# Splitting two mixer outputs during the attention, and another order of rows in the output projection

## The chip, the cores and the metric

The kernel runs on one core of a Trainium2 chip. The metric is the device time of one execution in microseconds (us). TensorE is PE in the views (its weight loads PEld), VectorE DVE, ScalarE ACT, GpSimd POOL, and SyncE, which issues most loads, SP.

## What is computed

A transformer of two layers over 512 tokens of width 1024, in float32. In each layer an input projection feeds three mixers: a sparse attention (512 columns), a gated delta net (256) and a convolution branch called conformer (256). Their outputs are joined and projected, and a mixture of 32 experts follows.

```
y_nsa  = _nsa(q, k_cmp, ..., gates, ...)
y_gdn  = _gated_deltanet(gdn_qkv, gdn_z, gdn_b, gdn_a, ...)
y_conf = _conformer_conv(conf_in, ...)
mix = jnp.concatenate([y_nsa, y_gdn, y_conf], axis=-1) @ w_out[l]
x = _layer_norm(DEEPNORM_ALPHA * x + mix, ln1_w[l], ln1_b[l])
moe = _hier_moe(x, ...)
x = _layer_norm(DEEPNORM_ALPHA * x + moe, ln2_w[l], ln2_b[l])
```

## The kernel before

Each layer has three stages. In the **mixer stage** the string `ORDER` gives the order in which the steps are written down: `k`, `c`, `q` are input projections, `w` to `z` prepare the queries of the four token tiles, `0` to `3` are their attention, `f` and `t` the conformer, and each `G` is one piece of the delta net, whose last pieces stand at the end. The **output projection** follows (L1104 to L1159), then routing and the **expert stage**, whose weights (6 MB for an expert) SP loads into rings of buffers. The experts are taken in an order that routing finds: the load of a routed expert needs its id, which SP reads from the tile `r_id` (L1247). Two experts are fixed and are loaded before.

Dependencies, semaphores and the order on each engine are not written by hand. A planner goes through the program and, by a model of the times, gives each engine its queue: of what is ready it takes what stands first in the program. On the chip each queue runs in that order. Tiles of one tag share a number of buffers, and a tile takes one when the planner comes to its first write and one is free. A pool that is opened where another one was closed waits for the old tiles that its own lie over.

The mixer outputs are four tiles of 128 x 1024: `mxA[0]` and `mxA[1]` (attention; token tiles 0 and 1, and 2 and 3), `mxC` (conformer, made in step `t`) and `mxG` (delta net). Products here are made of float32r halves: a value is split into a `hi` part by a cast on ACT and a `lo` part, the difference, by a subtraction on DVE (or POOL), and `mm3` (L354) makes three matmuls, hi x hi (L355), hi x lo (L356) and lo x hi (L357).

Before the projection a loop (L1105 to L1110) splits all four outputs. Its `hi` tiles (`mh`) lie in the pool `out`, and so do the six buffers for the split weights (`wo_hi`, `wo_lo`, tag `whl`); this pool takes over the space of the delta net's pool `g`, which is full of its 10 wide tiles (tag `g4`), the last of them `g_o`. The `lo` tiles (`ml`) take over buffers of the tags `cf` and `mxA`.

The projection then runs for two pairs of token tiles. Each goes through the 1024 rows of `w_out` in four quarters of 256 rows (`kq`), each a load of 1 MB on SP into a ring of three buffers, and each quarter in two parts of 128 rows, `k` = 2 `kq` and 2 `kq` + 1. A part is split (cast on ACT, L1132; subtraction on POOL for `k` in 1, 4, 7, else on DVE, L1133), and 12 matmuls follow: 2 token tiles x 2 halves of the columns x 3. Rows 0 to 511 (`k` 0 to 3) belong to the attention, `k` 4 and 5 to the delta net, 6 and 7 to the conformer. The quarters come in this order:

```
kq = (2, 3, 0, 1)[i]
```

so the delta net's rows are first. The sums lie in the banks of `opA` and `opB`; those of `opA` are the ones in which the delta net had `g_mix`, the transposes (L716) from which `mxG` is evacuated. After each pair come the residual with `xr`, a norm and the routing's logits.

The wide tiles of tag `x4` share six buffers: `cvt` (conformer), `kva0` and `kva1` (keys and values, read to the end of the attention), `kk` (compression), `q0` and `q1`, later the four `xr` (the residual, loaded on ACT's queue at L1115) and the two `xg` (gathered tokens, filled with zeros on POOL at L1198).

Of the kernel before, what the change touches and what calls it, by code (L numbers as in the profile page):

```python
# [21 lines left out]
D = 1024  # L22
NT = 4
P = 128
# [88 lines left out]
def hybrid_kernel(ctx, tc, x_in, w_in, w_out, cmp_pe, cmp_w1, cmp_w2, conv_w, a_log, dt_bias, norm_w,  # L113
# [191 lines left out]
    for l in range(layers):  # L305
# [492 lines left out]
        cvt = x4("cvt")  # L798
        for step in ORDER:
# [11 lines left out]
            elif step == 'k':  # L811

                kva = [x4(f"kva{i}") for i in range(2)]
# [34 lines left out]
            elif step == 'm':  # L848
# [7 lines left out]
                for kind in range(2):  # L856
# [3 lines left out]
                    if kind == 0:  # L860
                        kk = x4("kk")
# [33 lines left out]
            elif step == 'q':  # L895

                qq = [x4(f"q{i}") for i in range(2)]
# [18 lines left out]
            elif step == 't':  # L916
                mxC = conformer_tail(ca)
            elif step == 'r':
# [184 lines left out]

        mh, ml = [], []  # L1104
        for src, tag in ((mxC, "cf"), (mxA[0], "cf"), (mxA[1], "mxA"), (mxG, "mxA")):  # L1105
            hi, lo = tp("out", "mh", 4, dt=F32R), tp("mix", tag, 2, "ml", F32R)
            A.copy(hi, src)
            V.tensor_tensor(lo, src, hi.bitcast(F32), op=ALU.subtract)
            mh.append(hi)
            ml.append(lo)  # L1110
        mh, ml = [[m[i] for i in (3, 0, 1, 2)] for m in (mh, ml)]
        for pr in range(2):
# [4 lines left out]
            def lt(m, k, t):  # L1117
                if k < 4:
                    return m[2 + t // 2][:, (t % 2) * 512 + k * P:(t % 2) * 512 + (k + 1) * P]
                return m[(k - 4) // 2][:, (k % 2) * 512 + t * P:(k % 2) * 512 + (t + 1) * P]  # L1120

            ap = [bank2("opA"), bank2("opB")]
            for i in range(4):
                kq = (2, 3, 0, 1)[i]
                w = wring("w_out")
                nc.sync.dma_start(w.rearrange("p (k c) -> p k c", k=2),
                                  w_out[l, kq * 256:(kq + 1) * 256, :].rearrange("(k p) c -> p k c", p=P))
                for kk in range(2):
                    k = 2 * kq + kk
                    src = w[:, kk * 1024:(kk + 1) * 1024]  # L1130
                    hi, lo = tp("out", "whl", WL, "wo_hi", F32R), tp("out", "whl", WL, "wo_lo", F32R)
                    A.copy(hi[:, :1024], src)  # L1132
                    (G if k in (1, 4, 7) else V).tensor_tensor(lo[:, :1024], src, hi[:, :1024].bitcast(F32), op=ALU.subtract)  # L1133
                    for t in (2 * pr, 2 * pr + 1):
                        for n in range(2):
                            mm3(ap[t % 2][:, n, :], lt(mh, k, t), lt(ml, k, t), hi[:, n * 512:(n + 1) * 512],
                                lo[:, n * 512:(n + 1) * 512], i == 0 and kk == 0, i == 3 and kk == 1)
# [504 lines left out]
```

## Time and profile before

| | |
|---|---|
| three runs | 1964.27, 1965.96 (median), 1978.44 us |
| the profiled execution | 1966.44 us, its span 1964.7 us |
| busy share of the span | PE 89%, DVE 51%, ACT 29%, POOL 20% |
| mean TensorE clock granted | 0.923 of full speed |
| HBM read | 476 MB, 247 GB/s over the span |

The span goes from the first to the last instruction of the profiled execution; all times in the rows count from its start. Layer 0 has its output projection from 371 to 425 us, layer 1 from 1345 to 1400. In a timeline a row gives start, duration, engine, line, operation, the tiles written and read, and in brackets how long the engine had been idle and what ended that. PEclk is the granted clock of TensorE: 1.00 is 2.4 GHz, 0.50 is 1.2 GHz. Matmuls are pipelined: a row's 0.39 us is longer than the pitch at which rows follow each other.

### The profile page before, as it was taken

The numbers are of one execution on the slowest core, as the hardware profiler recorded it, in microseconds if no ns is written. First come the engines' busy times: TensorE is split into PE (matmuls) and PEld (weight loads), VectorE is DVE, ScalarE is ACT, GpSimd is POOL, SyncE is SP. The second block draws the span as 40 slices with busy tenths as digits, with TensorE's granted clock in tenths as the row PEclk, the third lists the DMA queues.
The fourth block names the chain that finished last, engine by engine and source line by source line (L and its number), as shares of the span: only waits on it lengthen the run. The fifth ranks groups of instructions, "written<-read, shape, count | busy, mean of one in ns | idle before, by whom it ended". The sixth has DMA issues, their size and how long they took to land. (4 is left out here: it accounts for less than half of the span.)

```text
span 1964.7 us, 31355 instructions
## 1 busy us (share of the span) xinstructions
PE 1743.3 (89%) x11812; PEld 1021.7 (52%) x11812; DVE 1009.4 (51%) x2258; ACT 573.8 (29%) x1250; POOL 387.3 (20%) x354
## 2 busy tenths in 40 slices
PE   8899699887988899999789987998799898999996
PEld 6776576672443434333377765666634434343333
DVE  2756867463533524343637659664644324244335
ACT  3332565432110112121233336553222101121122
POOL 2224641312200000000222356213131000000001
PEclk9997689988999899999999976998889998999998
DMA  5222000747999989999632210017489999799994
GB/s 179 87 86 76 12 12 12 264 152 284 408 402 405 403 323 383 409 374 409 249 110 82 90 64 2 12 43 267 138 320 409 402 403 405 305 399 408 362 409 181
DMA packets 147339, 478.41 MB, mean 244 GB/s; under 512 B 23032, under 2 KB 25584, under 8 KB 147184
## 3 DMA queue, kind: packets, MB, share of 16 engines
q1 hardware_dynamic: 138304, 456.74, 61.0%
q10 hardware_dynamic: 4144, 10.70, 1.5%
q0 software_dynamic: 4736, 8.92, 1.3%
q8 instruction: 95, 1.56, 0.3%
q14 instruction: 60, 0.49, 0.1%
HBM read 476.04 MB, written 8.39 MB: 247 GB/s over the span
## 5 line engine op out<-in xcount | busy, mean ns | idle before, releaser
L1282 PE MATMUL f_gu<-w_gu,m_xe 128*32 128x256 f32 (+1 forms) x3456 | 398.6, 454 | 19.9 <-DMA w_gu<-in_moe_w_up 17.8
L1282 PEld LDWEIGHTS f_gu<-w_gu,m_xe 128*32 128x32 f32 (+1 forms) x3456 | 134.9, 118 | 270.6 <-issue 222.5
L1314 PE MATMUL f_y<-w_d,f_hTs 128*32 128x256 f32 (+2 forms) x1824 | 258.1, 480 | 9.9 <-ACT f_hTs L1299 2.9
L1324 DVE TENSOR_TENSOR m_yl<-f_y,m_yh 32x256 fp32r<-32x256 f32 (+2 forms) x222 | 115.3, 520 | 263.8 <-ACT m_yh L1322 256.1
L1322 ACT CAST m_yh<-f_y 32x256 fp32r<-32x256 f32 (+2 forms) x222 | 98.4, 443 | 304.0 <-PE f_y L1314 301.7
L1374 POOL DMA_INDIRECT xg<-x1D,m_idx x34 | 35.9, 1056 | 744.3 <-PE f_hT L1297 331.2
L1314 PEld LDWEIGHTS f_y<-w_d,f_hTs 128*32 128x32 f32 (+2 forms) x1824 | 83.5, 126 | 162.0 <-issue 130.8
L1435 DVE TENSOR_TENSOR xr<-xr,m_sc 128x1024 f32<-128x1024 f32 x128 | 152.8, 1218 | 25.5 <-PE m_sc L1434 24.6
L1289 DVE SCALAR_TENSOR_TENSOR f_h<-f_h,m_wsl,f_gu 128x128 f32<-128x128 f32 (+1 forms) x76 | 33.0, 434 | 227.1 <-ACT f_h L1288 226.7
L1434 PE MATMUL m_sc<-m_yh,m_ohT 128*128 128x512 f32 (+1 forms) x256 | 114.7, 448 | 28.7 <-DVE xr L1435 28.5
L1288 ACT ACTIVATE f_h<-f_gu 128x128 f32<-128x128 f32 (+1 forms) x76 | 26.4, 348 | 383.1 <-PE f_gu L1282 289.5
L351 POOL TENSOR_TENSOR w_hl<-w_slice,w_hl 128x512 fp32r<-128x512 f32 (+1 forms) x54 | 70.3, 1302 | 254.4 <-ACT w_hl L350 247.0
L1434 PE MATMUL m_sc<-m_yl,m_ohT 128*128 128x512 f32 (+1 forms) x256 | 103.5, 404 | 0.0
L350 ACT CAST w_hl<-w_slice 128x512 fp32r<-128x512 f32 (+1 forms) x96 | 56.1, 589 | 150.2 <-PE ipB L357 123.9
L1278 PE MATMUL f_gu<-w_gu,m_xe 128*128 128x512 f32 x192 | 88.8, 607 | 0.4 <-DMA w_gu<-in_moe_w_gate 0.3
L1434 PEld LDWEIGHTS m_sc<-m_yh,m_ohT 128*128 128x128 f32 (+1 forms) x256 | 49.6, 194 | 65.5 <-DVE xr L1435 42.4
L766 POOL TENSOR_TENSOR cvt<-cvt,cv_t 128x485 f32<-128x485 f32 (+28 forms) x66 | 77.9, 1181 | 16.4 <-ACT cv_t L762 12.7
L1020 ACT ACTIVATE e<-a_s,a_nm 128x128 f32<-128x128 f32 (+3 forms) x128 | 66.5, 526 | 45.9 <-DVE a_nm L1015 38.7
L1417 PE MATMUL m_g<-ident,xg 128*128 128x128 f32 (+2 forms) x272 | 47.8, 299 | 19.4 <-DMA xg<-x1D,m_idx 16.1
L351 DVE TENSOR_TENSOR w_hl<-w_slice,w_hl 128x512 fp32r<-128x512 f32 (+1 forms) x42 | 30.0, 715 | 64.3 <-ACT w_hl L350 64.1
L1278 PEld LDWEIGHTS f_gu<-w_gu,m_xe 128*128 128x128 f32 x192 | 35.0, 191 | 53.2 <-issue 48.9
L1015 DVE TENSOR_REDUCE a_nm<-a_s 128x1 f32<-128x384 f32 (+3 forms) x88 | 55.0, 634 | 11.0 <-PE a_s L1012 10.2
(474 smaller groups left out, 3326.1 us busy)
## 6 DMA issues: line engine op xcount, KB each, us to landing
w_gu<-in_moe_w_gate SPq DMA_DIRECT2D x256, 512.0 KB, 12.1
w_gu<-in_moe_w_up SPq DMA_DIRECT2D x256, 512.0 KB, 12.7
w_d<-in_moe_w_down SPq DMA_DIRECT2D x128, 1024.0 KB, 12.1
w_slice<-in_w_in SPq DMA_DIRECT2D x20, 1024.0 KB, 5.2
w_out<-in_w_out SPq DMA_DIRECT2D x16, 1024.0 KB, 4.9
x1D<-xr SPq DMA_DIRECT2D x8, 512.0 KB, 3.3
w_slice<-in_w_in SPq DMA_DIRECT2D x4, 560.0 KB, 5.7
x<-in_x SPq DMA_DIRECT2D x4, 512.0 KB, 4.3
```

What stands on the lines that cost most here:

```text
L350: A.copy(hi[:, :n], src)
L351: (G if LOE(npc[0], k) else V).tensor_tensor(lo[:, :n], src, hi[:, :n].bitcast(F32), op=ALU.subtract)
L766: G.tensor_tensor(ac2[:, 30 - j:512], ac2[:, 30 - j:512], tm, op=ALU.add)
L1015: V.tensor_reduce(nm[:, 0:hb], ps[:, :hb * L].rearrange("p (h l) -> p h l", h=hb), axis=AX.X, op=ALU.max, negate=True)
L1020: A.activation(e[:, :L], ps[:, i * L:(i + 1) * L], AF.Exp, bias=nm[:, i:i + 1], accum_out=sums[:, i0 + i:i0 + i + 1])
L1278: T.matmul(pg[:, i, :], xe(k), wv[:, i, :], start=(k == 0), stop=(k == 7), skip_group_check=True)
L1282: T.matmul(pg[j * c:(j + 1) * c, 0, 0:2 * fw], xe(k), wv[:, :, j * fw:(j + 1) * fw], start=(k == 0), stop=(k == 7), skip_group_check=True)
L1314: T.matmul(o, lt, wv[:, n * nw:(n + 1) * nw], start=(k == 0), stop=(k == 3), skip_group_check=True)
L1322: A.copy(hi[:, n * nw:(n + 1) * nw], src[n])
L1324: V.tensor_tensor(lo[:, n * nw:(n + 1) * nw], src[n], hi[:, n * nw:(n + 1) * nw].bitcast(F32), op=ALU.subtract)
L1434: T.matmul(ps2[:, n, :], ohT[0:nr, t * P:(t + 1) * P], y[0:nr, n * 512:(n + 1) * 512], start=(i == 0), stop=(i == 1))
L1435: V.tensor_tensor(xr[t][:, :D], xr[t][:, :D], ps2.rearrange("p a b -> p (a b)"), op=ALU.add)
```

## The change

`mxC` and `mxA[0]` are split right after step `t`, in the middle of the attention. Their `hi` tiles are now of tag `x4` and take two of its six buffers; their `lo` tiles have the same buffers as before. The tiles `kk`, `q0`, `q1`, `kva0` and `kva1` are declared ahead of the steps. `mxA[1]` and `mxG` are split inside the first pair, after the first quarter, and the pool `out` keeps two `mh` buffers instead of four. The quarters now come in the order 3, 0, 1, 2: conformer, attention, delta net. `lt` finds the halves in the dictionary `mp`.

```diff
@@ -795,7 +795,18 @@
             return mxC
 
         mxA, QS, PCT = [], {}, {}
-        cvt = x4("cvt")
+
+        cvt, kk = x4("cvt"), x4("kk")
+        qq = [x4(f"q{i}") for i in range(2)]
+        kva = [x4(f"kva{i}") for i in range(2)]
+
+        def mix_parts(src, hi, tag):
+
+            lo = tp("mix", tag, 2, "ml", F32R)
+            A.copy(hi, src[:, :D])
+            V.tensor_tensor(lo, src[:, :D], hi.bitcast(F32), op=ALU.subtract)
+            return hi, lo
+
         for step in ORDER:
             if step == 'c':
 
@@ -810,7 +821,6 @@
                     V.scalar_tensor_tensor(u[i], u[i], 1.0, a0[:, i, :], op0=ALU.add, op1=ALU.mult)
             elif step == 'k':
 
-                kva = [x4(f"kva{i}") for i in range(2)]
                 kv = [kva[t // 2][:, (t % 2) * 512:(t % 2) * 512 + 512] for t in range(NT)]
                 a0, a1 = bank2("ipA"), bank2("ipB")
                 for k, hi, lo in pieces([(512, 1024)]):
@@ -857,8 +867,6 @@
                     w1 = wring("w_cmp")
                     nc.sync.dma_start(w1.rearrange("p (a c) -> p a c", c=P), cmp_w1[l, kind].rearrange("(a p) c -> p a c", p=P))
 
-                    if kind == 0:
-                        kk = x4("kk")
                     ps = bank("cmp_tr")
                     for t in range(NT):
                         T.transpose(ps[:, t * P:(t + 1) * P], kv[t][:, kind * P:(kind + 1) * P], ident)
@@ -894,7 +902,6 @@
 
             elif step == 'q':
 
-                qq = [x4(f"q{i}") for i in range(2)]
                 q = [qq[t // 2][:, (t % 2) * 512:(t % 2) * 512 + 512] for t in range(NT)]
                 a0, a1 = bank2("ipA"), bank2("ipB")
                 for k, hi, lo in pieces([(0, 512)]):
@@ -915,6 +922,7 @@
                 ca = conformer()
             elif step == 't':
                 mxC = conformer_tail(ca)
+                mp = {n: mix_parts(src, xp.tile([P, D], F32R, tag="x4", name="mh"), "cf") for n, src in (("C", mxC), (0, mxA[0]))}
             elif step == 'r':
 
                 w1c, b1c = [cp.tile([P, 8], F32, tag=n, name=f"{n}{l}") for n in ("w1c", "b1c")]
@@ -1100,31 +1108,26 @@
 
         xsrc = x_in[0] if l == 0 else x_res
         xr = []
-
-        mh, ml = [], []
-        for src, tag in ((mxC, "cf"), (mxA[0], "cf"), (mxA[1], "mxA"), (mxG, "mxA")):
-            hi, lo = tp("out", "mh", 4, dt=F32R), tp("mix", tag, 2, "ml", F32R)
-            A.copy(hi, src)
-            V.tensor_tensor(lo, src, hi.bitcast(F32), op=ALU.subtract)
-            mh.append(hi)
-            ml.append(lo)
-        mh, ml = [[m[i] for i in (3, 0, 1, 2)] for m in (mh, ml)]
         for pr in range(2):
             for t in (2 * pr, 2 * pr + 1):
                 xt = x4(f"xr{t}")
                 A.dma_start(xt[:, :D], xsrc[t * P:(t + 1) * P, :])
                 xr.append(xt)
-            def lt(m, k, t):
+            def lt(i, k, t):
                 if k < 4:
-                    return m[2 + t // 2][:, (t % 2) * 512 + k * P:(t % 2) * 512 + (k + 1) * P]
-                return m[(k - 4) // 2][:, (k % 2) * 512 + t * P:(k % 2) * 512 + (t + 1) * P]
+                    return mp[t // 2][i][:, (t % 2) * 512 + k * P:(t % 2) * 512 + (k + 1) * P]
+                return mp["GC"[(k - 4) // 2]][i][:, (k % 2) * 512 + t * P:(k % 2) * 512 + (t + 1) * P]
 
             ap = [bank2("opA"), bank2("opB")]
             for i in range(4):
-                kq = (2, 3, 0, 1)[i]
+
+                kq = (3, 0, 1, 2)[i]
                 w = wring("w_out")
                 nc.sync.dma_start(w.rearrange("p (k c) -> p k c", k=2),
                                   w_out[l, kq * 256:(kq + 1) * 256, :].rearrange("(k p) c -> p k c", p=P))
+                if pr == 0 and i == 1:
+                    for n, src in ((1, mxA[1]), ("G", mxG)):
+                        mp[n] = mix_parts(src, tp("out", "mh", 2, dt=F32R)[:, :D], "mxA")
                 for kk in range(2):
                     k = 2 * kq + kk
                     src = w[:, kk * 1024:(kk + 1) * 1024]
@@ -1133,7 +1136,7 @@
                     (G if k in (1, 4, 7) else V).tensor_tensor(lo[:, :1024], src, hi[:, :1024].bitcast(F32), op=ALU.subtract)
                     for t in (2 * pr, 2 * pr + 1):
                         for n in range(2):
-                            mm3(ap[t % 2][:, n, :], lt(mh, k, t), lt(ml, k, t), hi[:, n * 512:(n + 1) * 512],
+                            mm3(ap[t % 2][:, n, :], lt(0, k, t), lt(1, k, t), hi[:, n * 512:(n + 1) * 512],
                                 lo[:, n * 512:(n + 1) * 512], i == 0 and kk == 0, i == 3 and kk == 1)
 
             lg = osm("r_lg", [P, 2, 36])
```

## Rows read from the trace of the kernel before

**Rows 1.** The page: busy share of the 16 DMA engines in 40 slices.

```profile
...
DMA  5222000747999989999632210017489999799994
...
```

**Rows 2.** Timelines of DVE and SP at the end of the routing, layer 0.

```profile
...
442.07 0.17 DVE L1247 CAST r_id<-r_ids 1x32 int32<-1x32 f32 x1
...
443.42 0.37 SPq L1184 DMA_DIRECT2D w_gu<-in_moe_w_gate  x1
...
```

**Rows 3.** Timeline of PE around both output projections: start, us, instruction.

```profile
...
365.87 0.31 PE L932 MATMUL r_const<-wr,bb 128*128 128x36 f32 x2
371.00 0.80 PE L355 MATMUL opA<-wo_hi,mh 128*128 128x512 f32 x1 [4.82 <-ACT mh L1107]
...
373.35 0.79 PE L356 MATMUL opA<-wo_lo,mh 128*128 128x512 f32 x1 [1.13 <-POOL wo_lo L1133]
...
396.59 0.39 PE L357 MATMUL opB<-wo_hi,ml 128*128 128x512 f32 x1
...
1338.46 1.09 PE L716 MATMUL g_mix<-ident,g_o 128*128 128x128 f32 x8 [0.47 <-DVE g_o L712]
1344.52 0.80 PE L355 MATMUL opA<-wo_hi,mh 128*128 128x512 f32 x1 [4.96 <-ACT mh L1107]
...
1371.37 0.39 PE L357 MATMUL opB<-wo_hi,ml 128*128 128x512 f32 x1
...
```

**Rows 4.** Timeline of ACT at the same places.

```profile
...
365.63 0.59 ACT L239 COPY mxG<-g_mix 128x512 f32<-128x512 f32 x1 [4.59 <-PE g_mix L716]
366.12 1.05 ACT L1107 CAST mh<-mxC 128x1024 fp32r<-128x1024 f32 x1
...
369.90 1.04 ACT L1107 CAST mh<-mxG 128x1024 fp32r<-128x1024 f32 x1
...
1339.63 1.05 ACT L1107 CAST mh<-mxC 128x1024 fp32r<-128x1024 f32 x1
...
```

**Rows 5.** Timelines of ACT and DVE: inputs of the splits complete, and the last split.

```profile
...
281.88 0.59 ACT L239 COPY mxA<-a_o 128x512 f32<-128x512 f32 x1 [1.25 <-PE a_o L1042]
...
297.73 0.68 DVE L794 SCALAR_TENSOR_TENSOR mxC<-c_th,mxC 128x512 f32<-128x512 f32 x1
...
366.07 0.69 DVE L241 COPY mxG<-g_mix 128x512 f32<-128x512 f32 x1 [1.44 <-PE g_mix L716]
...
371.18 3.20 DVE L1108 TENSOR_TENSOR ml<-mxG,mh 128x1024 fp32r<-128x1024 f32 x1
...
```

**Rows 6.** Stretches: us, busy PE, PEld, DVE, ACT, POOL, then PEclk, DMA share, GB/s.

```profile
...
300.00:310.00 10.00, 10.00 (x91) 6.56 (x85) 5.22 (x13) 5.40 (x14) 1.15 (x2) 1.00 0.00 1
363.00:366.00 3.00, 3.00 (x27) 2.57 (x26) 0.69 (x1) 0.37 (x1) 0.00 (x0) 1.00 0.31 83
366.00:371.00 5.00, 0.18 (x4) 0.07 (x2) 4.49 (x6) 5.00 (x7) 0.92 (x1) 0.91 0.96 293
371.00:373.00 2.00, 1.22 (x2) 0.50 (x2) 1.90 (x2) 1.84 (x2) 2.00 (x1) 0.50 1.02 416
376.00:377.00 1.00, 1.00 (x4) 0.81 (x3) 0.66 (x1) 0.00 (x0) 0.00 (x0) 0.55 1.01 406
380.00:397.00 17.00, 16.98 (x75) 13.72 (x74) 5.51 (x5) 6.53 (x7) 6.08 (x3) 1.00 0.73 252
1265.00:1275.00 10.00, 10.00 (x113) 6.33 (x114) 4.05 (x9) 5.24 (x13) 1.15 (x2) 1.00 0.01 2
...
```

**Rows 7.** The tiles mh and w_out: ns min/median/max, first and last start.

```profile
...
L1107 ACT CAST mh<-mxA x4: 1043/1046/1047, 367.1 to 1341.5; 128x1024 fp32r<-128x1024 f32 x4
L1108 DVE TENSOR_TENSOR ml<-mxA,mh x4: 1225/1225/1226, 368.5 to 1343.4; 128x1024 fp32r<-128x1024 f32 x4
...
L1133 POOL TENSOR_TENSOR wo_lo<-w_out,wo_hi x12: 2378/2392/3231, 370.1 to 1385.4; 128x1024 fp32r<-128x1024 f32 x12
...
```

**Rows 8.** Line 1115, and the timeline of POOL, layer 1.

```profile
...
L1115 ACTq DMA_DIRECT2D xr<-in_x x4: 334/334/335, 181.7 to 318.0; - x4
...
1326.36 0.95 POOL L1198 MEMSET xg<- 128x1024 f32 x1 [4.32 <-PE a_o L1042]
...
```

## The prediction

> **What bounds the kernel now.** I read the page first. Its DMA line shows that most of each layer is the expert stage, in which the weight stream keeps the 16 DMA engines busy nine tenths and more; the low digits in between are the mixer stage, the output projection and the routing [rows 1]. The stream can't run through that gap: the load of the first routed expert is issued at 443.42 us, right after the cast of the expert ids at 442.07 [rows 2]. The ids come out of routing, routing out of the output projection. So a microsecond gained at the start of the projection should reach the end of the layer, and with two layers it counts twice.
>
> The timeline of PE gives the place. PE has its last work of the mixer stage at 366.2 us (365.87 + 0.31) and starts the projection at 371.00, having waited 4.82 us for a cast into `mh`; it waits another 1.13 for a POOL subtraction [rows 3]. Layer 1 repeats it: the last transposes of the delta net end at 1339.55, the projection starts at 1344.52. The timeline of ACT says why. From 366.12 to 370.94 it makes five casts of 1.05 us: three for `mh`, then one of the weights, then `mh` of `mxG`, which the first matmul needs because the order begins with the delta net's rows, k = 4 and 5 [rows 4]. Yet `mxA[0]` was complete at 282.5 and `mxC` at 298.4 [rows 5], and ACT had idled 4.59 us before 365.63 [rows 4]. The casts were late because their targets lie in the pool that takes over the delta net's space: they start as the delta net's last transposes end.
>
> The stretches add the clock. PEclk is 1.00 up to 366, 0.91 over 366 to 371, 0.50 over 371 to 373 and still 0.55 over 376 to 377; 380 to 397 runs at 1.00 with 75 matmuls in 16.98 us, 0.2264 us each, and without a gap [rows 6]. So from 380 on PE alone sets the pace, and the first pair of token tiles, 8 x 2 x 2 x 3 = 96 matmuls, is worth 96 x 0.2264 = 21.7 us. It took 396.8 - 371.0 = 25.8 in layer 0 and 1371.6 - 1344.5 = 27.1 in layer 1 (ends: 396.59 and 1371.37 plus one pitch) [rows 3].
>
> **The change part by part.** *The new start.* The first quarter is now k = 6 and 7, the conformer's. Their `hi` and `lo` exist since the attention, so the first matmul waits for one weight cast, `wo_hi` of k = 6. That tile still lies in the delta net's space, so the cast takes the place of the first `mh` cast: 366.12 + 1.05 = 367.2; in layer 1, 1339.63 + 1.05 = 1340.7 [rows 4]. The bank of `opA` was the delta net's; its second evacuation ends at 366.07 + 0.69 = 366.8 [rows 5], before that. The gain of the start is 3.8 us in each layer.
>
> *The rest of the first pair.* With PE fed and the clock up, 21.7 us follow. What can be late is a `lo` half of the weights. k = 6 has its on VectorE (the nearest row of that shape is 1.225 us), k = 7 and k = 1 on POOL, 2.39 us and up to 3.23 [rows 7]; the eight matmuls of a k that need no `lo` are 1.8 us of cover. Below, no stall; above, one whole POOL subtraction, 2.4 us. I take the stall that this same wait has now, 1.1 us [rows 3]. Layer 0: 367.2 + 21.7 + 1.1 = 390.0 instead of 396.8, gain 6.8. Layer 1: 1340.7 + 22.8 = 1363.5 instead of 1371.6, gain 8.1. Together 14.9 us.
>
> What the row shows of that wait: the last split on VectorE took 3.20 us where its shape takes 1.225, and POOL's subtraction beside it 3.23 instead of 2.39 [rows 5, 7]. The Trainium skill, "SBUF — State Buffer", section "SBUF: two separate sides", has VectorE operations with two SBUF inputs and GpSimd operations exclude each other for a whole instruction; the trace agrees, 3.20 being one 1.2 behind the rest of a 2.4. The change moves the splits of `mxA[1]` and `mxG` to just where POOL works on k = 7 and k = 1. By that rule alone the stall would be the upper end, 2.4 in each layer, and the time 2.6 us later.
>
> *The four splits.* The two late ones are 2 x 1.05 on ACT and 2 x 1.23 on VectorE [rows 7] behind the casts of k = 6 and 7; needed are `mxG` in the last quarter, 16 us on, and `mxA[1]` in the second pair, so they cost nothing beyond the stall above. The two early ones put 2.1 us on ACT and 2.45 on VectorE behind `mxC`. From 300 to 310 PE is busy 10.00 of 10, VectorE 5.22, ACT 5.40, and 1265 to 1275 is alike [rows 6]: PE is the bound and has the delta net and the attention to choose from. Queued behind them are exponentials and evacuations for which PE waits if they come late. Below: nothing (PE has no idle time there to win back). Above: all 4.55 us of a layer in the chain. I take 0.5, near the lower end, since the engines are half idle: 1.0 for both layers.
>
> *Buffers and queues.* The early `hi` tiles take two of the six wide buffers. Now four `xr` loads are issued on ACT's queue between 181.7 and 318.0 us [rows 8] into the buffers that `kk`, `cvt` and the two `q` leave; afterwards two of them have to wait for `kva`, which PE reads to the end of the attention. They are needed when the second pair ends, some 50 us later, so the lateness costs nothing; a wait in ACT's queue could (below). The two `xg` zero fills on POOL, which now take `kva`, wait until the projection is done with the early `hi` tiles; behind them stand weight subtractions, but `xg` itself is first needed by the gather after the ids. SP issues as many loads of `w_out` as before, in another order, each behind the same ring buffer; the fourth can go earlier. These edits I count as zero.
>
> *Sum.* 14.9 - 1.0 = 13.9 us. The profiled execution took 1966.44 (span 1964.7), 0.48 above the median of the three runs, 1965.96. From the median: **1952.1 us**, 0.7% less.
>
> **The rivals.** *The clock falls all the same.* For: it fell within the 4.8 us of waiting now, and was still low 5 us after PE had resumed [rows 6]. Against: PE will stand still 1.0 us, not 4.8. Price: what the first pairs lose now beyond 21.7 us, 4.1 and 5.4, less about 1.4 of stalls each: 6.7 for both. Time 1958.8. The Trainium skill, "TensorE: Matmul & The Clock Gate", section "HAM oscillation — how this bites in real kernels", warns that waits between bursts of matmuls bring the low clock back each time; the long wait here agrees with it, a 1 us wait at this place no row shows.
>
> *The splits aren't early or not ahead.* The instruction order is made by a planner; it can put `mxA[1]` and `mxG` before the weight casts (2.1 us a layer) or let the early splits hold up the attention (above 2 us a layer). About half of the gain goes: 1959.
>
> *Slower.* The `xr` loads that wait for `kva` block ACT's queue in the attention's last part, and the evacuations behind them hold PE. POOL shows such a wait now: its zero fill waited 4.32 us for that buffer [rows 8]. Two loads a layer at that price are 17.3 in both layers, so 1952.1 + 17.3 = 1969.4. It decides from 3.5 us a load; below that the change still wins. Against: the planner places them by the release it expects, and nothing needs them early.
>
> *More than forecast.* If PE went on at once, without stall or cost, the first pairs would end at 366.2 + 21.7 and 1339.55 + 21.7: gains of 8.9 and 10.3, time 1946.8. More needs a different order of the rest.
>
> **How the numbers follow.** Forecast (1946 to 1956) 0.62; clock 0.14; splits misplaced 0.12; slower mechanism 0.05; a reordered rest, faster than 1946.3, 0.07. The range 1944.5 to 1963 takes in the floor, the forecast and the two half gains with some microseconds for a shifted order elsewhere. About 1% (19.7 us) is what a measurement tells from no change: faster by more than that 0.08, within 0.88, slower 0.04.
>
> **What would show it.** Right: PE's wait before the first `opA` matmul falls from 4.82 to about 1 us and names a `wo_hi` cast; PEclk stays 1.00 after 366; the first pair takes 22 to 23 us; the casts of `mxC` stand near 300 and 1265 us; the first routed load moves from 443.4 to about 437. Wrong: PE starts at 367 but the clock is 0.50 there; PE idles on POOL's `wo_lo` for over 2 us; the delta net's last transposes come later than now; or the routed load moves by 7 us and the end doesn't.

## The result, and the profile after

| | before | after |
|---|---|---|
| median of 8 runs each | 1965.56 us (1954.08 to 1978.44) | 1948.54 us (1944.57 to 1954.53) |
| ratio | | 0.9912, interval 0.9889 to 0.9934 |
| the profiled execution | 1966.44, span 1964.7 | 1944.57, span 1942.8 |

The kernel is faster by 17.0 us, 0.9%; 13.9 were forecast, and the time lies in the forecast range. How it came about is another matter, and most of what follows is about that. The profiled execution of after is the fastest of its eight, so the 21.9 us between the two spans are more than the change is worth on the mean. Three executions among those of the experiments below, of 2231 to 2963 us at a mean granted clock of 0.59 to 0.72, stand in no ratio.

Layer 1 is the place to compare first, because the delta net ends last there in both kernels, as the forecast assumed. The timeline of PE after (columns as in [rows 3], its counterpart):

```profile
...
1323.17 1.07 PE L716 MATMUL g_mix<-ident,g_o 128*128 128x128 f32 x8
...
1325.42 0.50 PE L355 MATMUL opA<-wo_hi,mh 128*128 128x512 f32 x1
...
1326.80 0.50 PE L356 MATMUL opA<-wo_lo,mh 128*128 128x512 f32 x1 [0.64 <-DVE wo_lo L1136]
...
1329.24 0.39 PE L355 MATMUL opA<-wo_hi,mh 128*128 128x512 f32 x1
1329.47 0.39 PE L355 MATMUL opB<-wo_hi,mh 128*128 128x512 f32 x1
1331.48 0.50 PE L356 MATMUL opA<-wo_lo,mh 128*128 128x512 f32 x1 [1.63 <-POOL wo_lo L1136]
...
1348.39 0.50 PE L356 MATMUL opA<-wo_lo,mh 128*128 128x512 f32 x1 [2.68 <-POOL wo_lo L1136]
...
1355.23 1.15 PE L1151 MATMUL x1T_ps<-ident,xr 128*128 128x128 f32 x8
...
```

The start is as forecast: the wait of 4.96 us for a cast into `mh` is gone, and the projection begins 2.25 us after the last transposes begin, instead of 6.06. The timeline of ACT names the cast that lets it start (against [rows 4], where three `mh` casts came first):

```profile
...
1323.84 0.59 ACT L239 COPY mxG<-g_mix 128x512 f32<-128x512 f32 x1 [3.74 <-PE g_mix L716]
1324.32 1.05 ACT L1135 CAST wo_hi<-w_out 128x1024 fp32r<-128x1024 f32 x1
1325.27 1.05 ACT L806 CAST mh<-mxA 128x1024 fp32r<-128x1024 f32 x1
1326.22 1.05 ACT L806 CAST mh<-mxG 128x1024 fp32r<-128x1024 f32 x1
...
1339.50 1.05 ACT L1135 CAST wo_hi<-w_out 128x1024 fp32r<-128x1024 f32 x1 [1.78 <-PE opB L356]
...
```

It ends at 1324.32 + 1.05 = 1325.37, and PE starts at 1325.42. But the first pair then takes 29.7 us (its last matmul starts at 1354.89, and one pitch comes on top; the first `x1T` transpose follows at 1355.23), where the forecast had 21.7 + 1.1. Three waits are marked in the PE rows: 0.64, 1.63 and 2.68. The largest, on the way to the last quarter (k = 4 and 5), belongs to POOL, and POOL's timeline shows what it was doing:

```profile
...
1328.30 6.47 POOL L1136 TENSOR_TENSOR wo_lo<-w_out,wo_hi 128x1024 fp32r<-128x1024 f32 x2 [12.80 <-ACT wo_hi L1135]
1345.08 0.95 POOL L1201 MEMSET xg<- 128x1024 f32 x1 [10.31 <-PE opB L356]
1345.99 2.34 POOL L1136 TENSOR_TENSOR wo_lo<-w_out,wo_hi 128x1024 fp32r<-128x1024 f32 x1
```

The `wo_hi` cast of k = 4 ended at 1340.55. Its `lo` half is POOL's next job, but on POOL's queue the zero fill of `xg` stands in front of it, and that waits 10.31 us for PE's `opB` matmuls to be done with the buffer that it fills (of the wide tiles `opB` reads only the early `hi`). PE itself waits at 1348.39 for the subtraction behind the fill. The stretches add the clock (against [rows 6]):

```profile
...
1323.00:1345.00 22.00, 19.59 (x92) 15.62 (x93) 12.15 (x11) 10.58 (x11) 6.47 (x2) 1.00 0.98 367
1347.00:1353.00 6.00, 4.61 (x13) 3.70 (x14) 2.37 (x1) 0.67 (x2) 1.34 (x1) 0.72 0.55 182
1353.00:1356.00 3.00, 3.00 (x17) 2.29 (x17) 1.91 (x2) 1.31 (x2) 2.41 (x1) 1.00 0.00 0
402.00:408.00 6.00, 6.00 (x17) 4.74 (x18) 1.76 (x2) 1.13 (x2) 3.07 (x1) 0.61 0.58 167
...
```

It stays at 1.00 over the start, as forecast, and falls to 0.72 after the wait of 2.68 us. So the last 24 matmuls of the first pair take 10.0 us instead of 5.4. The whole pair takes 29.7 us, where layer 1 of before took 27.1, and most of the start's gain of 3.8 is given back.

In layer 0 the planner made another order: the delta net now ends 16 us ahead of the attention, and 30 matmuls of the projection stand between those of the attention. PE and ACT there:

```profile
...
344.80 1.04 PE L716 MATMUL g_mix<-ident,g_o 128*128 128x128 f32 x8
...
347.93 0.48 PE L355 MATMUL opA<-wo_hi,mh 128*128 128x512 f32 x1
...
361.12 0.65 PE L1050 MATMUL a_o<-a_pTs,kvb 128*64 128x256 f32 x4
...
380.29 1.16 PE L1151 MATMUL x1T_ps<-ident,xr 128*128 128x128 f32 x8 [0.18 <-DVE xr L1144]
...
400.25 0.80 PE L355 MATMUL opA<-wo_hi,mh 128*128 128x512 f32 x1 [3.38 <-ACT wo_hi L1135]
...
401.93 0.80 PE L356 MATMUL opA<-wo_lo,mh 128*128 128x512 f32 x1 [0.46 <-DVE wo_lo L1136]
...
```

```profile
...
396.36 0.21 ACT L1096 ACTIVATE r_s<-r_s 128x8 f32<-128x8 f32 x1 [5.88 <-DVE r_s L1095]
399.05 0.20 ACT L1098 ACTIVATE r_m<-r_m 128x2 f32<-128x2 f32 x1 [2.48 <-DVE r_m L1097]
399.16 2.92 ACT L1135 CAST wo_hi<-w_out 128x1024 fp32r<-128x1024 f32 x3
```

The first pair has no start to wait for: its matmuls begin while the attention still runs. The second has a new stall: three `wo_hi` casts stand on ACT behind the routing of the first pair (`r_s`, `r_m`), which waits 5.88 and 2.48 us for VectorE. PE waits 3.38 us for the first of them, the clock falls (0.61 over 402 to 408, in the stretches above), and 24 matmuls, with the wait ahead of them, take 12.6 us instead of 5.4.

The early splits are where the forecast put them (against [rows 7], where `mh` has its casts behind the delta net):

```profile
...
L806 ACT CAST mh<-mxC x1: 1048/1048/1048, 290.7 to 290.7; 128x1024 fp32r<-128x1024 f32 x1
L806 ACT CAST mh<-mxA x1: 1049/1049/1049, 291.7 to 291.7; 128x1024 fp32r<-128x1024 f32 x1
...
```

The load of the first routed expert goes out at 433.17 instead of 443.42 [rows 2]:

```profile
...
433.17 0.37 SPq L1187 DMA_DIRECT2D w_gu<-in_moe_w_gate  x1
...
```

That is 10.3 us, but 8.0 of them had been there at the conformer's end (its last transposes stand at 294.5 us in before, at 286.5 in after), and up to there PE has the same instructions in the same order in both kernels. A second trace of before, in the first experiment, has its last transposes of the conformer at 285.6 without any change: these 8 us are chance, and go with the granted clock. The other 2.3 us aren't in the second trace of after either, where the load goes out at 435.97 and the conformer's last transposes stand at 286.2.

### The profile page after: what moved, and what is told of

It reads as the page before. It is cut to its first block, busy times and chain, and to the rows that moved or that the text cites. A ratio compares the mean times of both kernels' runs of the same rounds, so it can differ in the third digit from the quotient of the medians.

```text
span 1942.8 us, 31345 instructions
## 1 busy us (share of the span) xinstructions
PE 1730.3 (89%) x11812; PEld 1016.1 (52%) x11812; DVE 1012.3 (52%) x2258; ACT 573.3 (30%) x1250; POOL 389.9 (20%) x354
## 5 line engine op out<-in xcount | busy, mean ns | idle before, releaser
L1317 PE MATMUL f_y<-w_d,f_hTs 128*32 128x256 f32 (+2 forms) x1824 | 252.5, 474 | 9.2 <-ACT f_hTs L1302 2.9
L1363 ACT ACTIVATE m_xe<-m_g,b1c,w1c 128x256 f32<-128x256 f32 (+3 forms) x72 | 37.2, 541 | 79.7 <-DVE m_xe L1365 79.5
```

The lines of the kernel that those rows point to most:

```text
L1317: T.matmul(o, lt, wv[:, n * nw:(n + 1) * nw], start=(k == 0), stop=(k == 3), skip_group_check=True)
```

## The experiments

Each kernel was compared with before on the same chip. The table has the traces of all of them, by four stages of a layer: from its first transpose to the end of the mixers (the later of attention and delta net; in brackets the projection's matmuls that PE had done by then), from there to the first `x1T` transpose, from there to the matmul of the expert ids, and on to the next layer or the end. Each number is the difference of two starts in the timeline of PE; the last goes to the end of the span.

| us | L0 mixers | to x1T | to ids | rest | L1 mixers | to x1T | to ids | rest | span |
|---|---|---|---|---|---|---|---|---|---|
| before | 360.1 | 32.6 | 44.1 | 541.7 | 355.1 | 33.9 | 44.1 | 548.3 | 1964.7 |
| again_before | 351.3 | 32.8 | 44.1 | 546.2 | 363.3 | 33.1 | 44.1 | 546.5 | 1966.0 |
| before_delta_first | 359.8 | 33.1 | 44.1 | 546.4 | 356.3 | 30.9 | 45.7 | 547.0 | 1968.2 |
| early_g_first | 352.8 | 28.4 | 50.3 | 545.9 | 356.3 | 30.8 | 44.1 | 546.9 | 1960.2 |
| late_c_first | 352.0 | 31.2 | 44.1 | 542.8 | 351.4 (2) | 25.5 | 50.4 | 544.2 | 1946.5 |
| late_c_first_reuse | 351.8 | 31.8 | 44.1 | 542.8 | 356.0 | 32.8 | 44.1 | 544.7 | 1953.4 |
| after | 356.4 (30) | 19.2 | 51.2 | 540.8 | 350.8 | 32.1 | 44.1 | 543.5 | 1942.8 |
| again_after | 358.9 (30) | 19.2 | 51.5 | 541.8 | 350.3 | 32.1 | 44.1 | 543.6 | 1946.2 |
| w_out_on_act_again | 358.1 (30) | 20.7 | 51.6 | 545.2 | 350.4 | 32.1 | 44.1 | 550.4 | 1957.6 |
| after_delta_first | 350.3 | 32.4 | 44.1 | 545.0 | 354.4 (32) | 22.3 | 50.3 | 545.3 | 1949.1 |
| after_lo_k7_on_dve | 356.7 (44) | 17.4 | 50.7 | 541.7 | 356.1 (44) | 17.4 | 49.1 | 545.1 | 1939.2 |
| after_reuse_w_out | 355.4 (30) | 19.6 | 44.0 | 544.5 | 352.8 (14) | 24.7 | 44.1 | 545.7 | 1935.8 |
| after_reuse_and_lo_k7 | 360.1 (44) | 17.0 | 44.3 | 540.6 | 344.3 | 26.9 | 44.1 | 543.6 | 1926.0 |

**Before and after once more** (no edit).

> The kernel before, unaltered, for a second profiled execution. In the first pair of traces 8.7 us of the 21.9 us between the two spans arise before 345 us of layer 0, where both kernels have the same instructions in the same order: the granted clock fell at about 121, 142 and 247 us in the trace of before and not in that of after. Theory 'chance of the clock': this second trace has its falls elsewhere or not at all, and at the delta net's last transposes of layer 0 (364.96 in the first) it lies anywhere from 356 to 366. Theory 'the change does it there too': it falls at the same three places again, and the transposes come at 364 to 366. Ratio to before 1.000 within 0.002.

> The kernel after, unaltered, for a second profiled execution and a second interval. Theory 'the gate' (the projection no longer waits for casts, and TensorE's clock is kept): 13 to 15 us faster than before. Theory 'chance of the clock' alone: under 8 us. Theory 'the change does it before the splits too': 20 us or more. The wait before the first matmul of opA of layer 1 stays under 1 us in the second trace too.

Measured: ratio 0.9991 (0.9958 to 1.0023) for before, 0.9893 (0.9848 to 0.9939; medians 1950.31 and 1966.27) for after. The first matmul of layer 1's projection waits for nothing in the second trace either. The gain is 16.0 us between the medians and 21.0 by the ratio, with 12 to 30 in its interval. That excludes "chance of the clock" alone (under 8), but it doesn't tell "the gate" (13 to 15) from "the change does it before the splits too" (20 or more). Against the latter stands the second trace of before, which has the early stretch as fast as after has it. The stretches of the first trace of before and of this second one, at two of the three falls of the clock:

```profile
...
120.00:124.00 4.00, 3.15 (x10) 2.67 (x11) 3.46 (x6) 2.33 (x4) 0.68 (x1) 0.61 0.73 197
142.00:147.00 5.00, 5.00 (x13) 3.93 (x13) 4.83 (x8) 0.58 (x1) 0.00 (x0) 0.50 0.37 143
...
```

```profile
...
120.00:124.00 4.00, 3.93 (x20) 3.33 (x21) 3.40 (x5) 2.96 (x5) 0.00 (x0) 1.00 0.86 249
142.00:147.00 5.00, 5.00 (x18) 3.22 (x16) 4.83 (x6) 0.62 (x1) 2.25 (x2) 0.90 0.00 0
...
```

The fall at 121 us is not there and that at 142 is mostly gone; at the third, 247 to 257 us, PEclk is 0.50 in the first trace and 1.00 in the second, and there 4.6 us of the difference arise. Layer 0's mixers take 351.3 us instead of 360.1, with the same instructions on PE in the same order. Of the five traces with that order of layer 0 or nearly that (before, again_before, before_delta_first, late_c_first, late_c_first_reuse) two have about 360 and three about 352. So 8 us of a single trace are chance. The two stages behind the mixers, to `x1T` and to the ids, repeat to 0.8 us in the two traces of a kernel and can be compared one by one. The rest doesn't: 541.7 and 546.2 us in layer 0 of before.

**The quarter order alone, and the early splits alone.**

The first edit is made in before, the second in after:

```diff
-                kq = (2, 3, 0, 1)[i]
+                kq = (3, 0, 1, 2)[i]
```

```diff
-                kq = (3, 0, 1, 2)[i]
+                kq = (2, 3, 0, 1)[i]
-                if pr == 0 and i == 1:
+                if pr == 0 and i == 0:
```

> Before, with the new order of the quarters alone (k = 6, 7, then 0 to 3, then 4, 5); all four splits stay behind the attention, in the delta net's old space. Theory 'the gate': the first opA matmul of layer 0 waits for the casts mh<-mxC and wo_hi, two casts of 1.05 us behind the delta net's last transposes, so it starts some 2.7 us earlier than now (371.0 in before), and the clock may fall or not: 4 to 9 us faster than before in both layers. Theory 'the order' (the gain is the delta net that ends 20 us ahead of the attention in layer 0, with the projection's matmuls in the attention's waits): no more than 3 us faster, since in layer 0 the delta net stays last.

> After, with the old order of the quarters (k = 4, 5, 6, 7, then 0 to 3) and so the splits of mxA[1] and mxG ahead of the first quarter; mxC and mxA[0] are still split early. Theory 'the gate': layer 1 has its wait for mh<-mxG back (3 to 5 us, and the clock's fall behind it), layer 0 not, because there mxG is ready before the attention ends: 5 to 9 us faster than before, 6 to 9 less than after. Theory 'the order': the delta net of layer 0 still ends ahead of the attention, and the gain stays within 3 us of that of after. Theory 'the early casts alone free ACT': as after, 15 to 17 us faster.

Measured: 0.9925 (0.9897 to 0.9954) for the order alone, 0.9968 (0.9938 to 0.9999) for the early splits alone. The first gives 14.7 us by its ratio (11.8 between the medians), more than either theory expected. The second gives 6.3 by its ratio (2.4 between the medians; the interval reaches from 0.2 to 12), as "the gate" said and far from after, so neither the early casts nor the delta net's place alone make the gain. The interval of the first overlaps with both of after: the runs don't show that the early splits add anything to the new order of the quarters. The start of late_c_first in layer 0, on ACT and PE:

```profile
...
358.09 1.05 ACT L1107 CAST mh<-mxC 128x1024 fp32r<-128x1024 f32 x1
359.04 1.99 ACT L1107 CAST mh<-mxA 128x1024 fp32r<-128x1024 f32 x2
360.93 1.04 ACT L1132 CAST wo_hi<-w_out 128x1024 fp32r<-128x1024 f32 x1
...
```

```profile
...
362.03 0.50 PE L355 MATMUL opA<-wo_hi,mh 128*128 128x512 f32 x1 [3.87 <-ACT wo_hi L1132]
...
364.24 0.79 PE L356 MATMUL opA<-wo_lo,mh 128*128 128x512 f32 x1 [1.29 <-DVE wo_lo L1133]
...
```

Its `wo_hi` cast stands behind three `mh` casts, not one, so PE still waits 3.87 us, and the way to `x1T` is only 1.4 to 1.6 us shorter than in before. The rest of its gain isn't in that stage of layer 0, and its shorter mixers there (352.0 us) have PE's order of before, so they are the chance seen above. In early_g_first the wait for `mh` is back in layer 1 (2.66 us), as "the gate" said. But both edits also changed the order of a whole stage: in late_c_first the attention of layer 1 and the projection overlap a little (2 matmuls), in early_g_first the delta net of layer 0 ends first, and both have a second pair of 50 us to the ids.

**The delta net first, with and without the change.**

```diff
-ORDER="GkGcomGqPwfx0yG1t2z3GGr"
+ORDER="GkGcomGqPwfx0yG1t2zGG3r"
```

> After, with the delta net's last two steps ahead of attention step 3 in the program instead of behind it. By its order layer 0 has the delta net last again, and it is layer 1 where the delta net ends first and projection matmuls stand between those of the attention. Theory 'the order' (the layer with that order gains): the stage from the conformer's end to the ids takes 148 us or less in layer 1 and 146 or more in layer 0, as before. Theory 'the gate' (what counts is that the projection isn't held up by casts): layer 0 takes 140 to 142 us, since the projection there starts at once behind the delta net with its casts done, and layer 1 about 148: 4 to 7 us below after. In both the whole is between 1940 and 1955.

> Before, with the same step order: by its order layer 0 stays as in before, and in layer 1 the delta net ends 34 matmuls ahead of the attention, so the splits of mxC, mxA[0] and mxG can be made while the attention still runs. No quarter is moved and no split is early. Theory 'the order': layer 1 takes 147 to 150 us from the conformer's end to the ids instead of 156, and the time is 6 to 9 us below before. Theory 'the gate': first matmul of the projection of layer 1 waits for nothing there too, so the same 4 to 8 us in layer 1, and nothing in layer 0; what tells the two apart is where: by 'the order' the time from the conformer's end to the end of the mixers falls from 78 us to about 72, by 'the gate' it stays and the time from there to the ids falls.

Measured: 0.9925 (0.9902 to 0.9947) and 0.9965 (0.9943 to 0.9988). after_delta_first is after with the layers' roles exchanged, and that shows what the overlap is worth together with the stalled second pair behind it: nothing. Layer 0, with the delta net last, has the rows of after's layer 1, the zero fill's wait of 10.31 us among them, and 32.4 us to `x1T`; layer 1, with the overlap, has the stalled second pair (50.3). Counting the overlapped matmuls at 0.2264 us [rows 6], an estimate, the way from the mixers' end to the ids is 32 x 0.2264 + 22.3 + 50.3 = 79.8 us with overlap and 76.5 without; before had 76.7 to 78.0. From the conformer's end to the ids, where nothing has to be estimated, it is 148.0 us with overlap and 147.3 without. What the overlap is worth with no stall behind it, this kernel doesn't show. By its stage numbers "the gate" falls (layer 0 was to take 140 to 142 us from the conformer's end to the ids, and took 147.3, the fill's stall of 4.7 us among them). "The order" named layer 1's number, 148.0, but after has 148.0 there with the other order. before_delta_first gains 6.9 us by its ratio, about what both expected, and doesn't decide where: its mixers of layer 1 take 76.5 us from the conformer's end, between the 72 and the 78 that were to tell the theories apart.

**The loads of `w_out` on another queue.**

```diff
-                nc.sync.dma_start(w.rearrange("p (k c) -> p k c", k=2),
+                A.dma_start(w.rearrange("p (k c) -> p k c", k=2),
```

> After, with the loads of w_out issued on ACT's queue instead of SP's, where they stand behind the prefetch of the static experts' weights and, in layer 0, the router weights of the next layer. From the conformer's last transposes to the matmul of the expert ids the traces so far take 147.1 and 147.3 us in layer 0 and 155.9 and 156.4 in layer 1 (before, two traces), 145.0 and 148.1, 148.0 and 148.1 (after). In after 24 matmuls of the second pair of layer 0 take 12.6 us where 5.4 is the rule, and the last 24 of the first pair of layer 1 take 10.1. Theory 'SP's queue' (w_out comes late because it is issued behind other loads): both stalls go, the stage takes about 139 us in layer 0 and 143.5 in layer 1, and the time is 8 to 13 us below after (1936 to 1942). Theory 'ring slot' (w_out waits for its buffer): the stage is within 2 us of after in both layers. Theory 'the DMA engines' (w_out shares them with the prefetch whatever the queue): some 3 to 5 us less than after.

> The kernel with w_out's loads on ACT's queue once more, for a profile at the chip's usual clock (the first was taken while TensorE was granted 0.59 on the mean). By its times it is 0.6% faster than before, so not faster than after, and theory 'SP's queue' can only hold if its gain is lost elsewhere: then the last quarter of the first pair of layer 1 takes about 5.4 us (10.1 in after) and the third of the second pair of layer 0 about 5.4 (12.6). Theory 'ring slot' or 'the DMA engines': those two still take 8 us or more, and the ACT casts wo_hi wait for a w_out load there.

Measured: 0.9939 (0.9916 to 0.9962). The trace is of w_out_on_act_again, a single execution of 1959.41 us. Both stalls are as they were, 10.0 and 12.9 us for 24 matmuls, and the kernel is no faster than after. ACT in layer 0:

```profile
...
399.94 0.21 ACT L1096 ACTIVATE r_s<-r_s 128x8 f32<-128x8 f32 x1 [5.43 <-DVE r_s L1095]
402.63 0.20 ACT L1098 ACTIVATE r_m<-r_m 128x2 f32<-128x2 f32 x1 [2.48 <-DVE r_m L1097]
402.74 2.92 ACT L1135 CAST wo_hi<-w_out 128x1024 fp32r<-128x1024 f32 x3
```

The three casts (k = 2, 3 and 4) follow `r_m` by 0.11 us, as in after, and they start without a wait of their own. Yet the load of the slice with k = 2 and 3 goes out at 377.63 here, 25.0 us ahead of `r_m`, and at 385.98 in after, 13.1 us ahead. So "SP's queue" falls, and for this stall so do "ring slot" and "the DMA engines", by which the casts were to wait for a load: what holds them is `r_m` in front of them. In layer 1 the zero fill is in front of the subtraction here too (PE waits 2.67 us for it).

**Fewer loads in the second pair.**

```diff
-                kq = (3, 0, 1, 2)[i]
-                w = wring("w_out")
+                kq = ((3, 0, 1, 2), (2, 1, 0, 3))[pr][i]
+                if pr == 0 or i == 3:
+                    ws[kq] = wring("w_out")
...
+                w = ws[kq]
```

> After, but the second pair takes the quarters in the reverse order (k = 4, 5, then 2, 3, then 0, 1, then 6, 7) and uses the three slices of w_out that still lie in the ring from the first pair, so that a layer loads five slices instead of eight. Theory 'w_out is late' (in the second pair too the wait is for a slice to arrive): the third quarter of the second pair of layer 0 takes 5.4 us instead of 12.6, the stage from the conformer's end to the ids 138 to 142 us in layer 0, and the time is 5 to 9 us below after. Theory 'the casts are late' (in the second pair of layer 0 the wo_hi cast stands on ACT behind the routing of the first pair, whatever arrives when): within 2 us of after. The first pair isn't helped by either: its last quarter in layer 1 stays near 10 us where the delta net ends last.

> The kernel with the new quarter order alone and all splits late, with the same reuse of three slices of w_out in the second pair. Its second pair had no long stall in layer 0 (5.4 us a quarter) and one of 17.7 in layer 1. Theory 'w_out is late': layer 1 gains, 1 to 4 us in all below the kernel without reuse (ratio to before 0.990 to 0.992), and since 6 MB less are loaded the static experts' weights come earlier, at no gain. Theory 'the casts are late': no difference, 0.9925 within 0.002.

Measured: 0.9851 (0.9811 to 0.9891, median 1937.89) on top of after, 0.9934 (0.9907 to 0.9962) on top of late_c_first, where no difference shows, as "the casts are late" said. Against after (0.9912 and 0.9893) it is worth 8 to 12 us, by ratios from different chips; its slowest execution, 1941.96, is faster than 13 of the 14 of after. The second pair of layer 0 takes 44.0 us to the ids instead of 51.2, and layer 1, which now has some overlap too (14 matmuls), no long quarter behind the first. ACT in layer 0 says how:

```profile
...
391.89 1.05 ACT L1137 CAST wo_hi<-w_out 128x1024 fp32r<-128x1024 f32 x1 [0.78 <-PE opB L356]
396.72 0.21 ACT L1096 ACTIVATE r_s<-r_s 128x8 f32<-128x8 f32 x1 [3.78 <-DVE r_s L1095]
396.84 1.03 ACT L1137 CAST wo_hi<-w_out 128x1024 fp32r<-128x1024 f32 x1
399.15 1.05 ACT L1137 CAST wo_hi<-w_out 128x1024 fp32r<-128x1024 f32 x1 [1.28 <-PE opB L356]
400.43 0.20 ACT L1098 ACTIVATE r_m<-r_m 128x2 f32<-128x2 f32 x1 [0.23 <-DVE r_m L1097]
```

The cast of k = 1 stands ahead of `r_s`, those of k = 6 and 7 between `r_s` and `r_m`; none waits for `r_m`. The slices lie in the ring, and with them there the planner made this order. The numbers of "w_out is late" were met for layer 0 (the third quarter takes 5.4 us), but by the rows it is the place of the casts in ACT's queue that changed. That the first pair's last quarter stays near 10 us was not tested, since no layer has the delta net last here.

**Another share of the subtractions for POOL.**

```diff
-                    (G if k in (1, 4, 7) else V).tensor_tensor(lo[:, :1024], src, hi[:, :1024].bitcast(F32), op=ALU.subtract)
+                    (G if k in (1, 3, 5) else V).tensor_tensor(lo[:, :1024], src, hi[:, :1024].bitcast(F32), op=ALU.subtract)
```

> After, with the subtractions wo_lo of k = 1, 3 and 5 on POOL instead of 1, 4 and 7, so that the first slice of w_out (k = 6, 7) is read by ACT and VectorE alone and its buffer comes free some 3 us earlier. Theory 'ring slot' (the fourth slice is fetched when the first slice's buffer is free): the last quarter of the first pair falls from 10 us to about 7 where the delta net ends last, and the time is 2 to 5 us below after. Theory 'the DMA engines' (the fourth slice waits behind the experts' prefetch): it stays at 9 to 10, and the time within 2 us of after. By its order, both layers have the delta net end ahead of the attention here: if that order is what gains, the layers take 145 to 148 us from the conformer's end to the ids.

> The reuse of three slices of w_out together with wo_lo of k = 1, 3 and 5 on POOL. By its order layer 0 has the delta net end ahead of the attention and layer 1 has it last, so layer 1 is the test that the kernel with the moved subtractions alone was not. Theory 'ring slot': in layer 1 the last quarter of the first pair takes 5.5 to 7 us (10.0 in after with the same order), from the end of the mixers to the first x1T transpose 27 to 29 us instead of 32.1, and the time is 1930 to 1938. Theory 'the DMA engines' (the fourth slice waits behind the experts' prefetch whenever its buffer comes free): the last quarter stays at 9 to 10 us and the time is 1938 to 1944. In both the second pairs take 44 us from x1T to the ids in both layers.

Measured: 0.9878 (0.9831 to 0.9924) alone and 0.9858 (0.9841 to 0.9874, median 1937.46) with the reuse. Alone it gives both layers the overlap, so it doesn't test the slot; from the conformer's end to the ids they take 144.2 and 142.6 us, under the 145 to 148 that the order was to give. With the reuse, layer 1 has the delta net last, and it is the forecast's case without the fill in the way. PE and POOL:

```profile
...
1313.65 0.50 PE L355 MATMUL opA<-wo_hi,mh 128*128 128x512 f32 x1 [0.20 <-ACT wo_hi L1137]
...
1314.97 0.50 PE L356 MATMUL opA<-wo_lo,mh 128*128 128x512 f32 x1 [0.59 <-DVE wo_lo L1138]
...
1318.57 0.50 PE L356 MATMUL opA<-wo_lo,mh 128*128 128x512 f32 x1 [0.61 <-DVE wo_lo L1138]
...
1335.54 0.50 PE L356 MATMUL opA<-wo_lo,mh 128*128 128x512 f32 x1
...
1338.28 1.17 PE L1153 MATMUL x1T_ps<-ident,xr 128*128 128x128 f32 x8 [0.15 <-DVE xr L1146]
...
```

```profile
...
1324.88 2.41 POOL L1138 TENSOR_TENSOR wo_lo<-w_out,wo_hi 128x1024 fp32r<-128x1024 f32 x1 [2.96 <-ACT wo_hi L1137]
1332.18 0.95 POOL L1203 MEMSET xg<- 128x1024 f32 x1 [4.89 <-PE opB L356]
1333.10 2.39 POOL L1138 TENSOR_TENSOR wo_lo<-w_out,wo_hi 128x1024 fp32r<-128x1024 f32 x1
...
```

The largest wait is 0.61 us, the quarters take 7.4, 5.6, 5.6 and 5.8, and `x1T` comes 26.9 us after the mixers' end, in the 27 to 29 of "ring slot". But POOL's rows give another cause than the ring, and in after itself the `wo_hi` cast of k = 4 was done at 1340.55, 7.8 us before PE went on, so its slice wasn't late. The fill still waits (4.89 us), now ahead of the subtraction of k = 5, while that of k = 4 is VectorE's. So PE has the 12 matmuls of k = 4 to do meanwhile, 2.7 us; the subtraction ends at 1333.10 + 2.39 = 1335.49, and PE takes it at 1335.54. Two edits stand together here, and the fill alone on another engine was not tried.

## Why the prediction was right, and where it was wrong

**The time** was forecast 3.6 us too high. **The account** behind it was wrong in its largest term, so that the time came out in the range is luck. The first pairs were to give 6.8 + 8.1 = 14.9 us. From the mixers' end to the ids, with the overlapped matmuls counted at 0.2264 us each, the means of the two traces are 76.8 and 77.6 us in before (layer 0, layer 1), 77.4 and 76.2 in after: 0.8 us together.

**The start** was right where its premise held: 3.8 us forecast, 6.06 - 2.25 = 3.8 measured in layer 1, by the cast that was named. In layer 0 the premise, that the delta net ends last, failed.

**The stall term** failed: "What can be late is a `lo` half of the weights", 1.1 us, at most 2.4. A `lo` half it was, but three waits sum to 4.95 in layer 1, and the clock fell behind the last: the prediction's own sign of being wrong, "PE idles on POOL's `wo_lo` for over 2 us". The first two, 0.64 and 1.63, are the kind that was bounded. The cover of eight matmuls wasn't there: two matmuls of k = 7 (1329.24 and 1329.47) stand ahead of the first that needs its `lo`, 0.46 us instead of 1.8. And POOL's two subtractions take 6.47 us together there, where one alone takes 2.40; VectorE's between them (k = 0, from 1329.20) takes 3.31 where 1.23 is usual. The Trainium skill, "SBUF — State Buffer", section "SBUF: two separate sides", whose exclusion of GpSimd and two-input VectorE operations was weighed at 2.4, fits that, and POOL's wait of 1.63, or 2.27 with the first, lies between the value that was worked out by it and the one taken.

**Buffers and queues** is the step that failed most plainly. It read: "The two `xg` zero fills on POOL [...] wait until the projection is done with the early `hi` tiles; behind them stand weight subtractions", and counted this as zero because `xg` itself is needed late. What is needed early is what stands behind it. The fill waited 10.31 us, and the last quarter took 10.0 or 10.1 us instead of 5.4 in all four layers that have the delta net last, the conformer first, the early splits and k = 4 on POOL (in after, again_after, w_out_on_act_again, after_delta_first). It took 5.4 in late_c_first's layer 0, whose fills run at 347 and 352 us, ahead of the projection, and 5.8 in after_reuse_and_lo_k7. The rival for "slower" did not come about: in layer 0 ACT issues the two late `xr` loads at 347.63 and 350.44, and the longest wait of ACT next to them is 1.82 us.

**The second pair** was taken as unchanged. It lost 7.1 to 7.4 us in layer 0 by the place of three casts on ACT.

**The clock** is half right: 1.00 over the start, and 0.72 behind the later wait. The early splits' 1.0 us can't be told from zero.

**What made up for it** was listed at 0.07, "a reordered rest", for times under 1946.3. Between the means of the two traces each, the mixers net of overlapped matmuls give 355.7 - 350.8 = 4.9 us in layer 0 and 359.2 - 350.6 = 8.6 in layer 1, the rests 2.7 and 3.8; with the 0.8 that is the 20.8 between the mean spans. Layer 0's part is no more than the chance shown above. Layer 1's is more: the seven traces with early splits and the conformer first have 344.3 to 350.8 us there net of overlap, the six others 350.9 to 363.3. The two traces of before have the same order on PE there and differ by 8.2 us, 355.1 at a mean granted clock of 0.893 and 363.3 at 0.862. At a like clock after takes 350.8 (0.892) and 350.3 (0.887), so 4 to 5 us of the 8.6 remain beside this chance. Which of the planner's moves gives them stays open. So does the rest: after's two traces are among the shortest, but the same stage took 550.4 us in w_out_on_act_again.

The runs, each with its span and mean granted clock, say in what form the gain comes. The eight of after have a mean span of 1947.1 us at a mean granted clock of 0.9295, and the product of the two, 1809.8 us, is that of before: 1810.5 to 1811.8 us in the four sets of 7 to 28 runs of before timed beside the experiments, at a clock of 0.921 to 0.922. So TensorE's clock is low for less of the time, and next to nothing else is saved. The account had about half of its gain from waiting saved at the start, 2 x 3.8 us, and that should have made the product smaller. No run isolates what keeps the clock up.

With the subtraction of k = 4 out of the fill's way the forecast's first pair exists: 26.9 us from the mixers' end to `x1T` in after_reuse_and_lo_k7 against 33.5 in before, 6.6 of the 8.1 forecast for layer 1. That kernel also loads less in the second pair.

## What to carry to other kernels

An instruction that waits longer than before costs what is queued behind it on its engine, not what its own result is worth: name the next instruction in that queue and who needs it, and give it a term. Where a planner orders the queues, one moved line can reorder a whole stage, so a sum over waits can come out right by accident: compare stage by stage, with two traces of each kernel, before believing it. Using data that still lies in a ring in reverse order gave 8 to 12 us on top of after and nothing on top of the new order alone, so its worth, too, seems to hang on the queues that the planner makes of it.

## What was not expected of the hardware

PE's waits of 0.64 and 1.63 us left the clock at 1.00; one of 2.68 was followed by 0.72 over the next stretch of 6 us and one of 3.38 by 0.61. And PE ran the same instructions of layer 0's mixers in the same order in 351.3 or in 360.1 us, at a mean granted clock of 0.917 or 0.882; the largest part of the difference, 4.6 us, arises at the fall at 247 us. Over whole executions, span times granted clock was the same to 2 us before and after a change that made the kernel 17 us faster.
